# Convolution taps over 1024 tokens instead of two halves, and the forget gate read out by ScalarE, in a one-core hybrid decoder block

## The chip, the core and the metric

The kernel runs on one core of a Trainium2 chip. Its engines work side by side, each through its own queue in order: TensorE (PE; its weight loads are listed as PEld), VectorE (DVE), ScalarE (ACT), GpSimd (POOL), and SyncE (SP), which issues most of the DMAs. The metric is the device time of one execution in microseconds, from 1157.99 to 1163.38 in three runs of the kernel before, with a median of 1163.02.

## What is computed

One layer, 1024 tokens by 1024 features, float32. The part that matters here is the first half of the layer:

```python
h = rms_norm(x, norm1_g)
proj = h @ w_in          # q 512 | k 512 | v 512 | fg 8 | conv_in 512 | pool_in 256
q, k = rms_norm(q per head), rms_norm(k per head)
fg = fg + b_f                                        # forget-gate logits
att = forgetting_attention(q, k, v, fg)              # cumsum(log_sigmoid(fg)) as a bias

a, b = split(conv_in)
c = a * sigmoid(b)                                   # 256 channels
c = causal_depthwise_conv(c, dw_w) + dw_b            # 31 taps
conv = silu(layer_norm(c)) @ pw_w
pool = multiscale_pool(pool_in, pool_w, pool_scale)  # trailing means over 2, 4, 8, 16
x = x + concat[att, conv, pool] @ w_out
```

A gated MLP with 2816 hidden features follows; it takes the larger part of the time and is not touched.

## The kernel before

Features lie on the 128 partitions and tokens along the free axis for the convolution and the pooling; tokens lie on the partitions for q, k, v and the gates. Each product is made of three matmuls of float32 values that were split into a high and a low part (`mm3`, lines 53 to 55). The splits are made by ScalarE (high part, line 48) and by VectorE or GpSimd (low part, line 49).

The first 245 us of the profile go like this:

- Up to about 77 us: loads and splits of the tokens, then the products for the convolution's and the pooling's inputs (512 tokens at a time, `feat_mm`), evacuated by VectorE (`feat_evac`, lines 171 to 182). The gated input of the convolution is `u`, two groups of 128 channels, with 30 zeros ahead of the tokens.
- Then six chunks of `w_in` against all tokens (`tok_chunks`, `tok_mm`): two for v (the second has the 8 gate columns too), then four for q and k. Each chunk has 8 token tiles, and each tile is 8 k blocks by three matmuls into one of four `mm` banks. In the loop over the tiles of chunk ci, `load_w` also loads and splits the weights of chunk ci + 2.
- Beside that, VectorE works at the side work: a generator, `side_work` (line 297), that yields after each step: the taps of channel groups 0 and 1 (`taps`), then the two halves of `conv_tail` (transposes of the finished taps `acc`, layer norm, transposes back, SiLU, split, pointwise product), then `pool_work` (running sums `pn`, then `d`, its split `dhl` and a product). The loops draw it by `step(n)`: 7 steps in each of the eight late feature halves, then 3 after each token tile of the first four chunks; what is left is drained ahead of the fifth.
- In the second chunk each tile's gate logits are read from the bank, scaled by `rstd` and given their bias by one VectorE instruction (line 433). `gate_cumsum` turns them into the cumulative sum `cumx`, which attention needs at its start (line 481).

Two pools are shared. The raw buffers (`rp`, five of them, `raw`) hold the raw weights `wr` of each `load_w`, and also the intermediate tiles of the side work: `y` and `sf` of the conv tails, `pn` and `d` of the pooling, `lf` and `cum` of the gates. The `tp` banks (two) serve the transposes and products of the side work.

The order on each engine is made by a scheduler at build time, from the order in which the code is written, from the dependencies, and from its own timeline. So a step that is drawn earlier is also placed earlier on its engines, and a buffer goes to whoever asks for it earlier in the code.

Of the kernel before, what the change touches and what calls it, by code (L numbers as in the profile page):

```python
# [11 lines left out]
AF = mybir.ActivationFunctionType  # L12
ALU = mybir.AluOpType
# [3 lines left out]
P = 128  # L17
S = 1024
D = 1024
NT = S // P  # L20
KT = D // P
H = 8
# [5 lines left out]
CW = 31  # L28
# [5 lines left out]
PC_G1, PC_CB, PC_LG, PC_LB, PC_PS = 0, 8, 10, 12, 14  # L34
PC_QG, PC_KG, PC_DW, PC_FW, PC_BF = 16, 17, 18, 80, 212
# [4 lines left out]
def tile_hybrid_block(ctx: ExitStack, tc: tile.TileContext, x: bass.AP, xT: bass.AP, prm: bass.AP,  # L40
                      g2: bass.AP, w_in: bass.AP, conv_pw: bass.AP, pool_w: bass.AP, w_out: bass.AP,
                      w_up: bass.AP, w_down: bass.AP, out: bass.AP):
    nc = tc.nc
# [19 lines left out]
    par = const.tile([P, PC_N], F32, name="par")  # L63
    nc.sync.dma_start(out=par, in_=prm)

    def pc(col):
        return par[:, col:col + 1]
# [22 lines left out]
    rstd = const.tile([P, NT], F32, name="rstd")  # L90
# [14 lines left out]
    def raw(shape, name):  # L105
        t = rp.tile([P, 1056], F32, name=name, tag="raw")
        return t[0:shape[0], 0:shape[1]]

    def mmps():
        return pmm.tile([P, 512], F32, name="mm", tag="mm")  # L110

    def tpps():
        return ptp.tile([P, 512], F32, name="tp", tag="tp")
# [18 lines left out]
    def load_w(k, c0, widths, lo=None):  # L132
        n = sum(widths)
        wr = raw((P, n), "wr")
        nc.sync.dma_start(out=wr, in_=w_in[k * P:(k + 1) * P, c0:c0 + n])
        o = 0
        for w in widths:
            t = wp.tile([P, 2, 272], F32R, name="w", tag="w")
            split(t[:, 0, 0:w], t[:, 1, 0:w], wr[:, o:o + w], lo)
            wt[(c0 + o, k)] = t  # L140
            o += w

    mcp = [mxa.tile([P, 4, 512], F32, name=f"mcp{g}", tag="mx") for g in range(2)]
    u = s8.tile([P, 2, 1056], F32, name="u", tag="s8")
    acc = s8.tile([P, 2, 1056], F32, name="acc", tag="s8")
# [8 lines left out]
    fgt = sp.tile([P, NT, H], F32, name="fgt", bufs=1)  # L154
# [92 lines left out]
                yield  # L247

    def taps(c):
        for half in range(2):  # L250
            o = half * 512
            a = acc[:, c, o:o + 512]
            nc.vector.tensor_scalar(out=a, in0=u[:, c, o:o + 512], scalar1=pc(PC_DW + c * CW),
                                    scalar2=pc(PC_CB + c), op0=ALU.mult, op1=ALU.add)
            yield
            for j in range(1, CW):
                nc.vector.scalar_tensor_tensor(out=a, in0=u[:, c, o + j:o + j + 512],  # L257
                                               scalar=pc(PC_DW + c * CW + j), in1=a, op0=ALU.mult, op1=ALU.add)
                yield

    def conv_tail(half):
        o = half * 512
# [34 lines left out]
    def side_work():  # L297
        yield from taps(0)
        yield from taps(1)
        yield from conv_tail(0)  # L300
        yield from conv_tail(1)
        yield from pool_work()
# [3 lines left out]
    def step(n):  # L306
        for _ in range(n):
            next(bg, None)
# [23 lines left out]
    for f in late:  # L332
        for half in range(2):
            ps = mmps()
# [20 lines left out]
    def tok_mm(c0, w, t):  # L355
        ps = mmps()
        ts = slice(t * P, (t + 1) * P)
        for k in range(KT):
            w_ = wt[(c0, k)]
            mm3(ps[:, 0:w], hhi[k][:, ts], hlo[k][:, ts], w_[:, 0, 0:w], w_[:, 1, 0:w], k == 0, k == KT - 1)  # L360
        return ps

    def gate_cumsum():
        fz = sp.tile([P, NT * H], F32, name="fz", bufs=1)
        z = fgt.rearrange("p t h -> p (t h)")
        nc.vector.scalar_tensor_tensor(out=fz, in0=z, scalar=-1.0, in1=z, op0=ALU.mult, op1=ALU.max)
        nc.scalar.activation(out=fz, in_=fz, func=AF.Exp, scale=-1.0)
        nc.vector.tensor_scalar(out=fz, in0=fz, scalar1=1.0, scalar2=None, op0=ALU.add)
        nc.scalar.activation(out=fz, in_=fz, func=AF.Ln)
        nc.vector.scalar_tensor_tensor(out=fz, in0=z, scalar=0.0, in1=fz, op0=ALU.min, op1=ALU.subtract)  # L370
        lf = raw((H, S), "lf")
        for half in range(2):
            ps = tpps()
            for j in range(4):
                t = half * 4 + j
                nc.tensor.transpose(out=ps[0:H, j * P:(j + 1) * P], in_=fz[:, t * H:(t + 1) * H], identity=ident)
            nc.vector.tensor_copy(out=lf[:, half * 512:half * 512 + 512], in_=ps[0:H, :])
        cum = raw((H, S), "cum")
        nc.vector.tensor_tensor_scan(out=cum, data0=lf, data1=lf, initial=0.0, op0=ALU.add, op1=ALU.min)
        nc.vector.memset(cumx.bitcast(F32), 0.0)  # L380
        nc.vector.tensor_copy(out=cumx[0:H], in_=cum)
        nc.vector.tensor_tensor(out=cumx[32:32 + H], in0=cum, in1=cumx[0:H].bitcast(F32), op=ALU.subtract)
# [33 lines left out]
    for ci, (c0, w) in enumerate(tok_chunks):  # L416
        if ci >= 2:
            dst = s8.tile([P, 2112], F32, name="qk", tag="s8")[:, 0:2048].rearrange("p (t c) -> p t c", t=NT)
            qk[ci % 2, (ci - 2) // 2] = dst
        if ci == 4:  # L420
            for _ in bg:
                pass
            pa2.close()
            qkp = qkp_ctx.enter_context(tc.tile_pool(name="qkp", bufs=3, **right))
            bg = prep_pair(0, tpps)
        for t in range(NT):
            ps = tok_mm(c0, w, t)
            if ci + 2 < len(tok_chunks):
                load_w(t, tok_chunks[ci + 2][0], (256,), nc.gpsimd)
            if ci < 2:  # L430
                nc.scalar.activation(out=vv[ci][:, t, :], in_=ps[:, 0:256], func=AF.Copy, scale=rstd[:, t:t + 1])
                if ci == 1:
                    nc.vector.scalar_tensor_tensor(out=fgt[:, t, :], in0=ps[:, 256:264],  # L433
                                                   scalar=rstd[:, t:t + 1],
                                                   in1=par[:, PC_BF:PC_BF + H], op0=ALU.mult, op1=ALU.add)
                step(3)
            else:
                sq = tp_.tile([P, DH], F32, name="sq")
                ss = tp_.tile([P, 4], F32, name="ss")
                for e in range(4):  # L440
                    nc.scalar.activation(out=sq, in_=ps[:, e * DH:(e + 1) * DH], func=AF.Square,
                                         scale=rstd[:, t:t + 1], accum_out=ss[:, e:e + 1])
                rsqrt(ss, ss, DH, 4)
                nc.gpsimd.tensor_scalar(out=ss, in0=ss, scalar1=rstd[:, t:t + 1], scalar2=None, op0=ALU.mult)
                nc.vector.tensor_tensor(out=dst[:, t, :].rearrange("p (h d) -> p h d", d=DH),  # L445
                                        in0=ps[:, 0:256].rearrange("p (h d) -> p h d", d=DH),
                                        in1=ss[:, :, None].broadcast_to([P, 4, DH]), op=ALU.mult)
                step(3 if ci < 4 else 1)
        if ci == 1:
            gate_cumsum()  # L450
# [587 lines left out]
```

## Time and profile before

| | |
|---|---|
| median of three runs | 1163.02 us |
| the profiled execution's own time | 1161.21 us |
| its span | 1159.4 us |
| granted TensorE clock, mean | 0.982 |
| taps (line 257), 120 instructions | 93.3 us busy on VectorE, 49.1 us to 161.0 us |
| first transpose of finished taps (line 267) | 155.0 us |
| first matmul of attention (line 481) | 245.0 us |

In the profile's rows stands first the start in us, then the length in us (in the merged view of time) or the groups' sums, then engine, line, operation, and the tile written, `<-`, the tiles read. `x6` says that six instructions are merged. In square brackets is the engine's idle time just before, and what ended it. A line of 48, 49 or 53 to 55 is that of a helper, so tiles say more than lines there.

### The profile page before, as it was taken

What the parts mean: (1) busy time and instruction counts of PE and PEld (TensorE: products, weight loads), DVE (VectorE), ACT (ScalarE), POOL (GpSimd) and SP (SyncE); (2) the same over time, 40 slices, a digit from 0 to 9 for tenths busy, and PEclk for the clock granted to TensorE, in tenths of its full rate; (3) what the DMA queues carried; (4) which work ended last, traced back from release to release, by engine and by line L of the source; (5) the groups of instructions that cost most, each with busy time, mean ns of one, the idle gap of its engine ahead of it and who ended that gap; (6) DMA issues with size and microseconds to landing.
All of it is one profiled execution on the core that took longest, in us unless ns stands there. A gap on an engine that the chain in (4) does not pass through costs nothing.

```text
span 1159.4 us, 15556 instructions
## 1 busy us (share of the span) xinstructions
PE 1104.9 (95%) x5684; PEld 921.4 (79%) x5684; DVE 882.5 (76%) x1259; ACT 576.0 (50%) x1045; POOL 361.4 (31%) x373
## 2 busy tenths in 40 slices
PE   7999889999999999879999999999999999899996
PEld 6789889978778878758888888888888788688875
DVE  5798974758998756778877888787878755998673
ACT  8322456688998644445443535353535343233331
POOL 1365597867666653101212121212121210000010
PEclk9999999999999999969999999999999999899999
DMA  9220110022111141211222121312221397672372
GB/s 359 72 81 25 40 28 20 15 74 74 55 48 46 47 154 73 109 37 55 89 75 96 68 96 68 105 59 85 79 98 67 117 328 267 240 263 91 128 235 74
DMA packets 51885, 119.99 MB, mean 103 GB/s; under 512 B 6368, under 2 KB 11872, under 8 KB 48992
## 3 DMA queue, kind: packets, MB, share of 16 engines
q1 hardware_dynamic: 46208, 99.06, 25.8%
q0 software_dynamic: 5600, 19.93, 4.3%
q8 instruction: 45, 0.74, 0.3%
q14 instruction: 32, 0.26, 0.1%
HBM read 94.84 MB, written 19.92 MB: 99 GB/s over the span
## 4 chain that ended last, share of the span: by engine, by line
PE 69%; DVE 10%; issue 7%; DMA 5%; ACT 4%; POOL 3%; SPq 1%; POOLq 0%; ACTq 0%; DVEq 0%
PE b L53 12%; PE b L55 12%; PE b L54 12%; PE mm L53 3%; PE mm L55 3%; PE mm L54 3%; DVE dl L49 3%; PE s L499 2%; DVE acc L257 2%; PE t L523 2%; DMA dr<-in_w_down_dram 2%; PE c L53 1%; PE c L55 1%; PE c L54 1%; DMA dr<-gd 1%
## 5 line engine op out<-in xcount | busy, mean ns | idle before, releaser
L814 POOL TENSOR_TENSOR ac<-ac 128x1024 f32<-128x1024 f32 x22 | 61.5, 2793 | 367.9 <-ACT u L795 207.3
L770 DVE SCALAR_TENSOR_TENSOR ac<-u,par,ac 128x1023 f32<-128x1023 f32 x88 | 112.7, 1280 | 9.6 <-ACT ac L768 8.7
L53 PE MATMUL mm<-w,hh 128*128 128x256 f32 (+1 forms) x384 | 110.3, 288 | 8.5 <-DVE qk L445 4.6
L54 PE MATMUL mm<-w,hh 128*128 128x256 f32 (+1 forms) x384 | 109.5, 285 | 0.6 <-POOL w L49 0.6
L55 PE MATMUL mm<-w,hl 128*128 128x256 f32 (+1 forms) x384 | 109.1, 284 | 0.0
L48 ACT CAST wsh<-ws 128x2048 fp32r<-128x2048 f32 x22 | 42.0, 1910 | 123.5 <-PE b L54 123.3
L257 DVE SCALAR_TENSOR_TENSOR acc<-u,par,acc 128x512 f32<-128x512 f32 x120 | 93.3, 835 | 0.0
L49 DVE TENSOR_TENSOR dl<-dr,dh 128x1024 fp32r<-128x1024 f32 (+1 forms) x39 | 65.6, 1684 | 28.0 <-ACT dh L48 24.9
L511 POOL TENSOR_TENSOR p<-p,l 128x896 f32<-128x896 f32 (+3 forms) x64 | 72.6, 1151 | 44.0 <-DVE l L510 37.5
L48 ACT CAST dh<-dr 128x1024 fp32r<-128x1024 f32 (+1 forms) x39 | 54.7, 1401 | 58.4 <-PE y L55 24.7
L53 PEld LDWEIGHTS mm<-w,hh 128*128 128x128 f32 x384 | 73.0, 190 | 10.1 <-DVE fgt L433 4.8
L49 POOL TENSOR_TENSOR w<-wr,w 128x256 fp32r<-128x256 f32 (+1 forms) x56 | 63.9, 1166 | 42.6 <-ACT w L48 42.3
L54 PEld LDWEIGHTS mm<-w,hh 128*128 128x128 f32 x384 | 73.1, 190 | 1.2 <-POOL w L49 0.8
L55 PEld LDWEIGHTS mm<-w,hl 128*128 128x128 f32 x384 | 73.2, 191 | 0.3
L864 POOL DMA_DIRECT2D out_dram<-acc x16 | 8.7, 542 | 206.9 <-DVE acc L860 206.3
L54 PE MATMUL x<-dl,dh 128*128 128x512 f32 x176 | 69.6, 395 | 3.4 <-DVE dl L49 3.4
L55 PE MATMUL x<-dh,dl 128*128 128x512 f32 x176 | 69.3, 394 | 0.0
L768 ACT ACTIVATE ac<-u,par 128x1024 f32<-128x1024 f32 x44 | 50.7, 1152 | 36.3 <-DVE u L805 35.8
L48 ACT CAST dh<-res 128x1024 fp32r<-128x1024 f32 x22 | 23.1, 1051 | 84.2 <-PE y L55 55.7
L49 DVE TENSOR_TENSOR wsl<-ws,wsh 128x2048 fp32r<-128x2048 f32 x22 | 50.4, 2290 | 12.4 <-ACT wsh L48 12.4
L677 DVE TENSOR_TENSOR ws<-wur 128x512 f32<-128x512 f32 x22 | 59.1, 2688 | 0.0
L53 PE MATMUL x<-dh 128*128 128x512 f32 x176 | 54.0, 402 | 5.2 <-DVE acc L860 4.5
(308 smaller groups left out, 3395.1 us busy)
## 6 DMA issues: line engine op xcount, KB each, us to landing
wur<-in_w_up_dram SPq DMA_DIRECT2D x22, 1024.0 KB, 4.9
dr<-in_w_down_dram SPq DMA_DIRECT2D x66, 256.0 KB, 5.1
dr<-gd SPq DMA_DIRECT2D x55, 256.0 KB, 4.3
gd<-ac POOLq DMA_DIRECT2D x22, 512.0 KB, 3.0
res<-gd SPq DMA_DIRECT2D x22, 256.0 KB, 5.6
wr<-in_w_in_dram SPq DMA_DIRECT2D x40, 128.0 KB, 2.1
v<-in_x_dram SPq DMA_DIRECT2D x8, 512.0 KB, 8.4
wor<-in_w_out_dram SPq DMA_DIRECT2D x16, 256.0 KB, 3.0
```

The costliest lines, as they stand in the source:

```text
L48: nc.scalar.copy(out=dst_hi, in_=src)
L49: (lo or nc.vector).tensor_tensor(out=dst_lo, in0=src, in1=dst_hi.bitcast(F32), op=ALU.subtract)
L53: nc.tensor.matmul(ps, a_hi, b_hi, start=first, stop=False, skip_group_check=more)
L54: nc.tensor.matmul(ps, a_hi, b_lo, start=False, stop=False, skip_group_check=more)
L55: nc.tensor.matmul(ps, a_lo, b_hi, start=False, stop=last, skip_group_check=more)
L257: nc.vector.scalar_tensor_tensor(out=a, in0=u[:, c, o + j:o + j + 512], scalar=pc(PC_DW + c * CW + j), in1=a, op0=ALU.mult, op1=ALU.add)
L499: nc.tensor.matmul(ps[:, 0:c1 - c0], qT[:, i * P:(i + 1) * P], part[:, c0:c1], start=b == 0, stop=b == 1 and c1 < n)
L511: nc.gpsimd.tensor_tensor(out=pt[:, 0:n], in0=pt[:, 0:n], in1=l[:, 1:2].broadcast_to([P, n]), op=ALU.mult)
L677: nc.vector.tensor_tensor(out=out, in0=a, in1=b, op=ALU.subtract)
L768: nc.scalar.activation(out=ac, in_=us, func=AF.Copy, scale=pc(w0 + 2))
L770: nc.vector.scalar_tensor_tensor(out=ac[:, j:S], in0=us[:, 0:S - j], scalar=pc(w0 + 2 - j), in1=ac[:, j:S], op0=ALU.mult, op1=ALU.add)
L814: nc.gpsimd.tensor_tensor(out=a[:, 1], in0=a[:, 1], in1=a[:, 0], op=ALU.mult)
```

## The change

The taps of a channel group run over all 1024 tokens at once: one bias step and 30 tap steps for each group, so 62 yields where there were 124. The steps that the loops draw stay as they were. The gate logits are read out by ScalarE without the bias, and `gate_cumsum` adds the bias for all 8 tiles in one VectorE instruction.

```diff
     def taps(c):
-        for half in range(2):
-            o = half * 512
-            a = acc[:, c, o:o + 512]
-            nc.vector.tensor_scalar(out=a, in0=u[:, c, o:o + 512], scalar1=pc(PC_DW + c * CW),
-                                    scalar2=pc(PC_CB + c), op0=ALU.mult, op1=ALU.add)
+        a = acc[:, c, 0:S]
+        nc.vector.tensor_scalar(out=a, in0=u[:, c, 0:S], scalar1=pc(PC_DW + c * CW), scalar2=pc(PC_CB + c),
+                                op0=ALU.mult, op1=ALU.add)
+        yield
+        for j in range(1, CW):
+            nc.vector.scalar_tensor_tensor(out=a, in0=u[:, c, j:j + S], scalar=pc(PC_DW + c * CW + j), in1=a,
+                                           op0=ALU.mult, op1=ALU.add)
             yield
-            for j in range(1, CW):
-                nc.vector.scalar_tensor_tensor(out=a, in0=u[:, c, o + j:o + j + 512],
-                                               scalar=pc(PC_DW + c * CW + j), in1=a, op0=ALU.mult, op1=ALU.add)
-                yield
...
     def gate_cumsum():
         fz = sp.tile([P, NT * H], F32, name="fz", bufs=1)
+        nc.vector.tensor_tensor(out=fgt, in0=fgt, in1=par[:, None, PC_BF:PC_BF + H].broadcast_to([P, NT, H]),
+                                op=ALU.add)
...
                 if ci == 1:
-                    nc.vector.scalar_tensor_tensor(out=fgt[:, t, :], in0=ps[:, 256:264],
-                                                   scalar=rstd[:, t:t + 1],
-                                                   in1=par[:, PC_BF:PC_BF + H], op0=ALU.mult, op1=ALU.add)
+                    nc.scalar.activation(out=fgt[:, t, :], in_=ps[:, 256:264], func=AF.Copy, scale=rstd[:, t:t + 1])
```

Three places show how the order on the engines moves. The first is VectorE, from the last evacuations of the pooling's input (`pu`) to the end of the taps. Before, the unbroken run of 36 half steps was followed by one gate readout after another with four half steps between them:

```order
L181 TENSOR_TENSOR pu<-mm,rb 128x512
L257 SCALAR_TENSOR_TENSOR acc<-u,par,acc 128x512 x7
L181 TENSOR_TENSOR pu<-mm,rb 128x512
L257 SCALAR_TENSOR_TENSOR acc<-u,par,acc 128x512 x36
L433 SCALAR_TENSOR_TENSOR fgt<-mm,rstd,par 128x8
L257 SCALAR_TENSOR_TENSOR acc<-u,par,acc 128x512 x4
L433 SCALAR_TENSOR_TENSOR fgt<-mm,rstd,par 128x8
```

Now the same place has 36 full steps (the lines are those of the changed file), then the bias add, the last five full steps, and at once the layer norm of the first conv tail:

```order
L181 TENSOR_TENSOR pu<-mm,rb 128x512
L255 SCALAR_TENSOR_TENSOR acc<-u,par,acc 128x1024 x36
L363 TENSOR_TENSOR fgt<-fgt,par 128x64
L255 SCALAR_TENSOR_TENSOR acc<-u,par,acc 128x1024
L366 SCALAR_TENSOR_TENSOR fz<-fgt 128x64
L255 SCALAR_TENSOR_TENSOR acc<-u,par,acc 128x1024
L368 TENSOR_SCALAR fz<-fz 128x64
L255 SCALAR_TENSOR_TENSOR acc<-u,par,acc 128x1024
L370 SCALAR_TENSOR_TENSOR fz<-fgt,fz 128x64
L255 SCALAR_TENSOR_TENSOR acc<-u,par,acc 128x1024 x2
L268 BN_STATS st<-tp 128x6 x2
```

The full steps of the two channel groups alternate in the run of 36; the last five are all of group 1. The conv tail came, before, only after six tiles of q had been evacuated.

The second place is TensorE at the third chunk (the first of q), whose weights are `w_825` (k block 0), `w_859`, `w_893` and so on. Before, the chunk's first tile went through its k blocks without a break, and so did six more before the first transpose of taps:

```order
L53 MATMUL mm_1375<-w_825,hh_0_117 128x256
L54 MATMUL mm_1375<-w_825,hh_0_117 128x256
L55 MATMUL mm_1375<-w_825,hl_0_125 128x256
L53 MATMUL mm_1375<-w_859,hh_1_118 128x256
L54 MATMUL mm_1375<-w_859,hh_1_118 128x256
L55 MATMUL mm_1375<-w_859,hl_1_126 128x256
```

Now four tiles (`mm_1572`, `mm_1612`, `mm_1652`, `mm_1692`) go through k blocks 0 to 2, and then come the transposes of the first conv tail (`tp<-acc`), k block 3 (`w_958`), and the tail's transposes back:

```order
L53 MATMUL mm_1692<-w_893,hh_2_119 128x256
L265 MATMUL tp_898<-ident_70,acc_136 128x128
L265 MATMUL tp_909<-ident_70,acc_136 128x128
L54 MATMUL mm_1692<-w_893,hh_2_119 128x256
L55 MATMUL mm_1692<-w_893,hl_2_127 128x256
L265 MATMUL tp_898<-ident_70,acc_136 128x128
L265 MATMUL tp_909<-ident_70,acc_136 128x128
L265 MATMUL tp_920<-ident_70,acc_136 128x128 x2
L265 MATMUL tp_962<-ident_70,acc_136 128x128 x2
L53 MATMUL mm_1572<-w_958,hh_3_120 128x256
L53 MATMUL mm_1612<-w_958,hh_3_120 128x256
```

Both conv tails and the first pooling product now stand among the first four tiles of the chunk; the fifth tile comes behind them. Before, they were spread from the third chunk to the sixth.

The third place is SyncE's queue with the raw weights of the third chunk, k blocks 3 to 7, and the semaphores that each load waits for. Before:

```order
L135 DMA wr_925<-in_w_in_dram 128x256 [waits DMAHW5_49,Pool_49]
L135 DMA wr_959<-in_w_in_dram 128x256 [waits DMAHW6_49,Pool_49]
L135 DMA wr_993<-in_w_in_dram 128x256 [waits DMAHW7_49,Pool_49]
L135 DMA wr_1027<-in_w_in_dram 128x256 [waits DMAHW0_49,Pool_49]
L135 DMA wr_1061<-in_w_in_dram 128x256 [waits DMAHW1_49,Pool_49]
```

Now:

```order
L135 DMA wr_956<-in_w_in_dram 128x256 [waits DMAHW6_49,Pool_49]
L135 DMA wr_1018<-in_w_in_dram 128x256 [waits DMAHW1_49,Pool_49]
L135 DMA wr_1077<-in_w_in_dram 128x256 [waits DMAHW5_49,DVE_49,PE_49]
L135 DMA wr_1141<-in_w_in_dram 128x256 [waits DMAHW7_49,DVE_49]
L135 DMA wr_1200<-in_w_in_dram 128x256 [waits DMAHW4_49,Pool_49]
```

The loads of k blocks 5 and 6 wait for VectorE and TensorE, whose tiles of the conv tail (`y`, `sf`) hold the raw buffers, where all waited for GpSimd's splits before. From attention's first matmul on, the order of every engine is the same but for a few rows.

## The prediction

> **What bounds the kernel now.** I read the busy times, then the stages, then what TensorE waits for, then single instructions around the convolution.
>
> ```profile
> PE 1104.9 (95%) x5684; PEld 921.4 (79%) x5684; DVE 882.5 (76%) x1259; ACT 576.0 (50%) x1045; POOL 361.4 (31%) x373
> ```
>
> TensorE is the bound: 95% of the 1159.4 us span. The execution took 1161.21 us, 1.8 below the median of 1163.02; I work against 1161.2 and add nothing for that difference. Only a change that makes TensorE wait less, or more, can move the time. All that the diff touches lies in the first 245 us, so the stages there come next.
>
> ```profile
> core 0: us, PE busy (x) PEld busy (x) DVE busy (x) ACT busy (x) POOL busy (x), PEclk, DMA share, GB/s
> 77.63:100.60 22.97, 22.39 (x187) 22.18 (x186) 22.97 (x33) 5.20 (x13) 6.22 (x6) 1.00 0.07 19
> 100.60:125.00 24.40, 21.82 (x179) 21.55 (x178) 19.42 (x33) 4.51 (x12) 15.33 (x8) 1.00 0.17 44
> 140.00:155.00 15.00, 12.35 (x92) 11.97 (x91) 14.54 (x28) 8.65 (x39) 11.78 (x14) 0.89 0.01 2
> 190.00:240.00 50.00, 49.55 (x396) 48.25 (x395) 35.14 (x67) 33.38 (x136) 36.92 (x56) 1.00 0.07 17
> ```
>
> Each stage row gives its length, then each engine's busy time, the granted clock and the DMA share. From 77.63 us on TensorE multiplies tokens by six weight chunks, 8 token tiles each, while VectorE runs the taps beside it (22.97 of 22.97 us busy). TensorE itself loses little; the view of waits for 77 to 240 us says to whom:
>
> ```profile
> PE mm L53 <- DVE qk L445: 4.6, 2, 2.7
> PE mm L53 <- DVE fgt L433: 4.0, 3, 2.6
> PE tp L267 <- DVE y L275: 1.4, 1, 1.4
> ```
>
> Total, times and longest: 10.0 us together.
>
> **The change, part by part.** First the taps: 124 steps of 512 tokens become 62 of 1024.
>
> ```profile
> 48.16 0.99 DVE L253 TENSOR_SCALAR acc<-u,par 128x512 f32<-128x512 f32 x2
> ...
> 73.29 6.51 DVE L257 SCALAR_TENSOR_TENSOR acc<-u,par,acc 128x512 f32<-128x512 f32 x6
> ...
> 86.53 23.93 DVE L257 SCALAR_TENSOR_TENSOR acc<-u,par,acc 128x512 f32<-128x512 f32 x36
> ...
> 564.38 1.28 DVE L770 SCALAR_TENSOR_TENSOR ac<-u,par,ac 128x1023 f32<-128x1023 f32 x1
> 565.57 0.68 DVE L784 TENSOR_TENSOR u<-u,b 128x512 f32<-128x512 f32 x1
> ...
> 569.03 2.60 DVE L770 SCALAR_TENSOR_TENSOR ac<-u,par,ac 128x1023 f32<-128x1023 f32 x2
> ```
>
> A half step costs 23.93 / 36 = 0.665 us. The same operation on 1023 elements lets its successor start after 1.19 us (564.38 to 565.57), or takes 1.30 where the second needs the first (2.60 / 2). Two bias steps of halves take 0.99; I leave the one that replaces them at that, and a range of a few tenths for it is lost in the rest. So a full tap saves 2 x 0.665 - 1.19 = 0.14 us, some 8 us of VectorE work over 60 steps. VectorE isn't the bound, so this is worth nothing by itself.
>
> What counts is the place. The side work is drawn by a counted number of steps, and its conv tails now come 62 steps earlier in the program. The rows of the order show it: from the first bias step up to the long unbroken run there were 35 half steps, 35 x 0.665 = 23.3 us, and are now 19 full ones, 19 x 1.19 = 22.6; the rest there is alike. So the run still begins near 86 us. It has 36 steps, before and now, but full ones: 36 x 1.19 = 42.8 us, to about 129 instead of 110.5. Behind it stand the bias add on the gates and five more full steps of one channel, each needing the one before: 5 x 1.30 = 6.5.
>
> GpSimd comes into this too.
>
> ```profile
> 73.46 9.34 POOL L49 TENSOR_TENSOR w<-wr,w 128x256 fp32r<-128x256 f32 x8 [5.56 <-ACT w L48]
> 99.55 11.52 POOL L49 TENSOR_TENSOR w<-wr,w 128x256 fp32r<-128x256 f32 x1 [16.75 <-ACT w L48]
> ```
>
> Eight weight splits beside taps go one to one with them: a tap then takes 6.51 / 6 = 1.085 us, 0.42 more than alone. But the split that comes up at 99.55, in the middle of the unbroken run, ends only at 111.07, just after that run's end at 110.46. So with full steps (i) the eight splits for the first chunk take some 8 x 0.52 = 4.2 us longer, and (ii) the splits of the third chunk's first weights, ready near 105 us, wait until the run ends near 129. Three of them among the last five taps add 3 x 0.42 = 1.3.
>
> ```profile
> 127.81 0.47 ACT L431 ACTIVATE v<-mm,rstd 128x256 f32<-128x256 f32 x1 [0.68 <-PE mm L55]
> ...
> 159.90 1.09 DVE L257 SCALAR_TENSOR_TENSOR acc<-u,par,acc 128x512 f32<-128x512 f32 x1
> ```
>
> TensorE finished the second chunk at 127.8. Without the gate wait (2.6) and with the 4.2 of (i) that is 129.4 now, which the gate add needs: VectorE goes on near 130. **Taps end**: 130 + 6.5 + 1.3 = 138 us, against 161 before. Bounds: 135 (129 + 5 x 1.19, no sharing) and 142 (another 4 us of sharing).
>
> That is earlier, yet TensorE now stands in front of it. In the order, after the third chunk's first three k blocks of four tiles (34 small matmuls, 4 us), the next rows of TensorE are transposes of the finished taps; then k blocks 3 to 7 alternate with both conv tails. The loads of blocks 5 and 6 wait for VectorE and TensorE work of the first tail, since its intermediate tiles sit in the same five buffers as the raw weights. Both loads, and every load behind them in SP's queue, come that much later. Before, all loads of this chunk waited for GpSimd alone, and TensorE had 168 small matmuls of the chunk to do ahead of the first such transpose, and whole tiles between the parts of a tail. Now it does both tails with only 62 small matmuls among them, and the chain of a tail is bare.
>
> ```profile
> 189.25 0.38 PE L267 MATMUL tp<-ident,acc 128*128 128x128 f32 x2
> 199.85 0.49 PE L282 MATMUL tp<-ident,y 128*128 128x128 f32 x3
> 208.52 0.39 PE L55 MATMUL tp<-s__2019,cw_hl 128*128 128x512 f32 x1
> ...
> 211.02 0.68 DVE L294 COPY mcp<-tp 128x512 f32<-128x512 f32 x1
> ...
> 213.33 1.14 ACT L48 CAST dhl<-d 128x512 fp32r<-128x512 f32 x2 [0.41 <-DVE pn L223]
> ...
> 215.27 1.29 DVE L49 TENSOR_TENSOR dhl<-d,dhl 128x512 fp32r<-128x512 f32 x2
> ```
>
> The second tail of before took 189.25 to 211.70, 22.4 us, with readouts of q and k between its parts. My estimate without those is 16: transposes to the last normalised tile 7.5 (9.7 in the rows up to 198.9), transposes back 1, SiLU and split 3, twelve products at 0.23 and the copies 4.5. Upper end 22.4, lower end 13. The second tail can't overlap the first: its transposes need the two banks which the first one's copies release. Then TensorE stands at the first pooling product, whose splits came 7.7 us behind the tail's last product (208.9 to 216.6); I take 5, since the running sums are now begun beside the tail, ends 3 and 7.7. So TensorE gets to the fifth tile of the third chunk at 138 + 32 + 5 = **175 us**.
>
> Where was that point before?
>
> ```profile
> 87.26 0.47 ACT L431 ACTIVATE v<-mm,rstd 128x256 f32<-128x256 f32 x1 [2.38 <-PE mm L55]
> ...
> 98.67 0.48 ACT L431 ACTIVATE v<-mm,rstd 128x256 f32<-128x256 f32 x1 [2.38 <-PE mm L55]
> ...
> L481 PE MATMUL f<-cumx,sel x16: 387/497/498, 245.0 to 355.0; 64*128 64x512 f32 x16
> ```
>
> Five readouts, 87.26 to 98.67, are 4 tiles: 2.85 us each. Attention began at 245.0. From the fifth tile on 28 tiles remain, 79.8 us, and with some 5 for 24 transposes and 8 products that is 85. So before, the same work was done by 160. **The delay is 175 - 160 = 15 us.** The 10.0 us of waits of before is inside the 160, so it has not to be taken off again. Behind this point the orders of all engines agree but for a few rows, so I carry the 15 to the end.
>
> A stop also slows what follows it.
>
> ```profile
> 490.00:500.00 10.00, 4.04 (x14) 2.83 (x15) 9.74 (x14) 7.08 (x8) 0.00 (x0) 0.50 0.00 1
> 500.00:510.00 10.00, 6.12 (x15) 4.24 (x15) 10.00 (x10) 4.45 (x5) 0.00 (x0) 0.50 0.00 0
> ```
>
> Where TensorE was busy 4.04 and 6.12 of 10 us, its granted clock was 0.50. Of TensorE's work in the new gap some 6 us lie on the chain (two times 12 products at 0.23 are 5.5). Half of it at half clock adds 3, all of it 6; I take 3, ends 0 and 6.
>
> [...]
>
> The gate readout: TensorE's bank is now freed by ScalarE alone, and the bias add waits for the eighth read; the five taps stand behind it on VectorE, and TensorE waits for those. ScalarE gets 8 small reads, VectorE loses 8 of 0.216 us and gets one add. I have no row of a 128x8 read on ScalarE; the ends are 0 and the 0.47 us of the 256 wide one, and I take 0.3. It hides in the 2.38 us for which ScalarE waits before each readout; uncovered it would cost 8 x 0.3 = 2.4. The 4.0 us for which TensorE waited on the gate readout goes, but taps and tails are late next, so it is worth nothing.
>
> Sum: 1161.2 + 15 + 3 = **1179**.
>
> **The rivals.** (1) *Faster.* The side work is out of the way early, so that waits go: 4.0 for the gates, 4.6 for q and k, 1.4 for the tail, which would give 1161.2 - 10 = 1151. It decides where TensorE gets to the fifth tile of the third chunk: by 160 there is no loss, by 150 the whole gain. For it speaks that the waits on q and k came beside taps; against it that the taps alone can't end before 135, and that two tails in line behind them leave 12 us each. Chance 0.08. (2) *No difference.* Tails of 13, taps at 135, pooling at 3 give 164, a delay of 4: 1165; or the change shortens VectorE's work and moves nothing else, 1161, which the order speaks against. Chance 0.15. (3) *Worse than my forecast.* Tails at the full 22.4 give 175 + 13 = 188 and 1192; what speaks against it is that no q and k readouts stand between the parts. It is counted inside the forecast's case, at about 0.1 of its 0.77.
>
> **How the numbers follow.** Forecast 1179, chance 0.77. A measurement of this kernel tells about 0.5% from no change, 5.8 us: faster is under 1157.2, slower over 1168.8. The lower end takes in the short tails, 1161.2 + 3 = 1164; the upper end is the long tails, 1192.
>
> **What would show it.** The full step near 1.28 us long; the taps' run from 86 to 129; a GpSimd split of over 20 us in it; taps ending near 138; TensorE waiting from about 130 on for splits, then for the normalised tiles and for pooling's split, 25 to 30 us in all between 125 and 180; clock below 1 there; attention's first matmul at 245 + 18 = 263 instead of 245. If TensorE reaches attention before 250, the tails weren't bare and I am wrong; if it does so at 263 and the end isn't later by the same amount, something behind has absorbed it.

## The result and the profile after

The changed kernel takes 1189.84 us in the median of 4 runs (1186.90 to 1190.16), the kernel before, in the runs beside it, 1162.10: a ratio of 1.0239, with a 95% interval of 1.0208 to 1.0271. It is slower by 27.7 us, where 18 were forecast. The profiled execution took 1189.61 us, with a span of 1187.8 and a mean granted clock of 0.971 (0.982 before).

The page of the profile, busy times and the groups that the change touches (busy us, mean ns of one | idle before them):

```profile
PE 1116.1 (94%) x5684; PEld 929.7 (78%) x5684; DVE 868.8 (73%) x1190; ACT 576.1 (49%) x1053; POOL 372.9 (31%) x373
...
L49 POOL TENSOR_TENSOR w<-wr,w 128x256 fp32r<-128x256 f32 (+1 forms) x56 | 84.3, 1527 | 43.2 <-ACT w L48 42.9
L255 DVE SCALAR_TENSOR_TENSOR acc<-u,par,acc 128x1024 f32<-128x1024 f32 x60 | 80.1, 1388 | 0.1
```

VectorE has 13.7 us less to do than before (882.5), and GpSimd's splits take 20.4 us longer (63.9 before) for the same 56 instructions. The merged view of time, VectorE, then GpSimd, shows why (start, length, instruction, idle before it):

```profile
84.58 43.13 DVE L255 SCALAR_TENSOR_TENSOR acc<-u,par,acc 128x1024 f32<-128x1024 f32 x36
127.64 0.21 DVE L363 TENSOR_TENSOR fgt<-fgt,par 128x64 f32<-128x64 f32 x1
...
133.24 2.60 DVE L255 SCALAR_TENSOR_TENSOR acc<-u,par,acc 128x1024 f32<-128x1024 f32 x2
```

```profile
72.18 12.49 POOL L49 TENSOR_TENSOR w<-wr,w 128x256 fp32r<-128x256 f32 x8 [4.18 <-ACT w L48]
100.87 29.92 POOL L49 TENSOR_TENSOR w<-wr,w 128x256 fp32r<-128x256 f32 x3 [16.20 <-ACT w L48]
139.79 0.72 POOL L49 TENSOR_TENSOR w<-wr,w 128x256 fp32r<-128x256 f32 x1
...
167.62 3.84 POOL L49 TENSOR_TENSOR w<-wr,w 128x256 fp32r<-128x256 f32 x1 [5.41 <-ACT w L48]
```

The run of 36 full steps lasts from 84.58 to 127.7, and no split that starts within it ends before it is over: three splits take 29.92 us, the first of them alone 27.57, to 128.44, where one takes 0.72 with no tap beside it. The taps end at 135.84. The stages behind them (length, busy time of PE, PEld, DVE, ACT, POOL, then granted clock, DMA share, GB/s):

```profile
130.00:140.00 10.00, 7.20 (x36) 6.96 (x37) 7.45 (x13) 2.09 (x4) 2.42 (x7) 0.67 0.05 13
140.00:150.00 10.00, 6.78 (x29) 5.59 (x30) 3.83 (x9) 4.37 (x7) 2.97 (x6) 0.67 0.10 24
150.00:160.00 10.00, 6.51 (x32) 5.21 (x31) 4.43 (x12) 0.41 (x1) 2.25 (x6) 0.84 0.01 5
160.00:170.00 10.00, 6.48 (x34) 5.60 (x34) 6.97 (x13) 2.78 (x5) 4.42 (x6) 0.83 0.05 13
170.00:180.00 10.00, 6.07 (x18) 4.85 (x18) 4.47 (x9) 5.14 (x28) 6.15 (x8) 0.66 0.15 39
180.00:190.00 10.00, 9.68 (x61) 8.78 (x62) 8.94 (x17) 5.53 (x21) 9.55 (x12) 0.83 0.26 66
```

From 130 to 180 TensorE is busy 33 of 50 us, at a clock of 0.66 to 0.84. What it waits for between 77 and 275 us (total, times, longest):

```profile
PE mm L54 <- POOL w L49: 10.4, 6, 3.2
PE tp L265 <- DVE y L273: 5.3, 2, 2.7
PE tp L53 <- ACT s__980 L48: 2.9, 1, 2.9
```

These are GpSimd's splits, the normalised tiles of the tails and the SiLU splits of the first tail: the bare chain of the tails, and weights that come late among them. The first matmuls of the fifth tile of the third chunk, and those of attention:

```profile
182.42 0.41 PE L53 MATMUL mm<-w,hh 128*128 128x256 f32 x1
```

```profile
L479 PE MATMUL f<-cumx,sel x16: 387/494/498, 271.0 to 380.8; 64*128 64x512 f32 x16
```

Attention begins 26.0 us later than before (245.0), and the end comes 28.4 later by the two profiled executions.

### The profile page after: what moved, and what is told of

It is laid out like the page before. It is cut to its first block, busy times and chain, and to the rows that moved or that the text cites. A ratio compares the mean times of both kernels' runs of the same rounds, so it can differ in the third digit from the quotient of the medians.

```text
span 1187.8 us, 15502 instructions
## 1 busy us (share of the span) xinstructions
PE 1116.1 (94%) x5684; PEld 929.7 (78%) x5684; DVE 868.8 (73%) x1190; ACT 576.1 (49%) x1053; POOL 372.9 (31%) x373
## 4 chain that ended last, share of the span: by engine, by line
PE 66%; issue 18%; DVE 6%; ACT 4%; POOL 3%; DMA 2%; SPq 0%; POOLq 0%; ACTq 0%; DVEq 0%
PE b L53 12%; PE b L55 12%; PE b L54 12%; PE mm L54 4%; PE mm L53 4%; PE mm L55 4%; PE s L497 2%; PE t L521 2%; POOL w L49 2%; PE c L53 1%; PE c L55 1%; PE c L54 1%; PE f L53 1%; PE f L55 1%; PE f L54 1%
## 5 line engine op out<-in xcount | busy, mean ns | idle before, releaser
L54 PE MATMUL mm<-w,hh 128*128 128x256 f32 (+1 forms) x384 | 112.1, 293 | 10.4 <-POOL w L49 10.4
L49 POOL TENSOR_TENSOR w<-wr,w 128x256 fp32r<-128x256 f32 (+1 forms) x56 | 84.3, 1527 | 43.2 <-ACT w L48 42.9
L54 PEld LDWEIGHTS mm<-w,hh 128*128 128x128 f32 x384 | 75.6, 197 | 11.9 <-POOL w L49 11.6
L255 DVE SCALAR_TENSOR_TENSOR acc<-u,par,acc 128x1024 f32<-128x1024 f32 x60 | 80.1, 1388 | 0.1
L53 PEld LDWEIGHTS mm<-w,hh 128*128 128x128 f32 x384 | 74.7, 197 | 4.3 <-DVE qk L443 3.3
L55 PEld LDWEIGHTS mm<-w,hl 128*128 128x128 f32 x384 | 75.6, 197 | 0.1
L766 ACT ACTIVATE ac<-u,par 128x1024 f32<-128x1024 f32 x44 | 50.7, 1152 | 31.2 <-DVE u L803 30.7
```

The source lines that it names most:

```text
L49: (lo or nc.vector).tensor_tensor(out=dst_lo, in0=src, in1=dst_hi.bitcast(F32), op=ALU.subtract)
L53: nc.tensor.matmul(ps, a_hi, b_hi, start=first, stop=False, skip_group_check=more)
L54: nc.tensor.matmul(ps, a_hi, b_lo, start=False, stop=False, skip_group_check=more)
L55: nc.tensor.matmul(ps, a_lo, b_hi, start=False, stop=last, skip_group_check=more)
L255: nc.vector.scalar_tensor_tensor(out=a, in0=u[:, c, j:j + S], scalar=pc(PC_DW + c * CW + j), in1=a, op0=ALU.mult, op1=ALU.add)
L766: nc.scalar.activation(out=ac, in_=us, func=AF.Copy, scale=pc(w0 + 2))
```

## The experiments

Three theories stood at the start. **D**: the conv tails, drawn earlier, lie bare in front of TensorE. **P**: the full steps themselves cost the time, since they shut GpSimd out for longer. **G**: the gate readout on ScalarE costs it. The first round showed that D alone isn't enough and brought a fourth, **S**, below. All times are medians; "before" is the kernel before in the same session; "splits moved" means that the low parts of the third chunk's weights are made on VectorE instead of GpSimd.

| kernel | taps | gate readout | tails drawn | us | before | ratio (95%) |
|---|---|---|---|---|---|---|
| the change | full | ScalarE | early | 1189.84 | 1162.10 | 1.0239 (1.0208 to 1.0271) |
| e1 | half | ScalarE | as before | 1176.62 | 1159.60 | 1.0143 (1.0128 to 1.0158) |
| e2 | full | VectorE | early | 1180.06 | 1159.60 | 1.0169 (1.0152 to 1.0186) |
| e3 | full | ScalarE | as before | 1173.70 | 1159.60 | 1.0109 (1.0089 to 1.0130) |
| e4 | half | VectorE | early | 1196.72 | 1159.60 | 1.0310 (1.0290 to 1.0330) |
| e6 | half | ScalarE, VectorE reads too | as before | 1161.76 | 1161.21 | 1.0003 (0.9990 to 1.0016) |
| e7 | half | ScalarE, splits moved | as before | 1156.86 | 1161.21 | 0.9957 (0.9939 to 0.9975) |
| e8 | full | VectorE | as before | 1161.75 | 1161.21 | 0.9995 (0.9978 to 1.0013) |
| e9 | full | ScalarE, splits moved | early | 1186.65 | 1161.21 | 1.0218 (1.0196 to 1.0240) |
| e10 | half | VectorE, splits moved | as before | 1161.23 | 1161.30 | 1.0001 (0.9990 to 1.0013) |
| e11 | full | ScalarE, splits moved | as before | 1158.15 | 1161.30 | 0.9986 (0.9971 to 1.0001) |
| e12 | the change, tail tiles in place | ScalarE | early | 1181.55 | 1161.30 | 1.0175 (1.0153 to 1.0197) |
| e14 | e11, tail tiles in place | ScalarE, splits moved | as before | 1170.61 | 1160.14 | 1.0096 (1.0078 to 1.0113) |

### The parts of the change, one by one

**e1** makes only the second and third hunk of the diff: half steps, gate readout on ScalarE, bias added once.

> The gate readout on ScalarE with its bias added once; the taps stay in halves, and the order of the conv tails stays that of the kernel before. Theory D (the conv tails are drawn 62 steps too early, so that both tails and the first pooling product stand bare between four tiles of the third chunk): this edit has no part in the loss; 1156 to 1163 us, since at most the 4.0 us of gate waits can go. Theory G (the gates on ScalarE, and the bias add that waits for the last of them in front of taps, make the loss): about 1180 or more.

Measured 1176.62, 17 us over the kernel before. This was the surprise: the part of the change that I had held for worth nothing costs more than half of the whole loss, though the tails are drawn where they were before.

**e2** makes only the first hunk: full taps, the old gate readout.

> Taps over 1024 tokens, with the old gate readout on VectorE. The order of the conv tails is that of the changed kernel. Theory D: the whole loss or a little more, 1186 to 1194 us, since gate readouts now wait behind full steps. Theory G: near 1163.

1180.06: slower by 20.5 us, and 6 us below the lower end of what D expected.

**e3** is the changed kernel with an empty draw behind every tap, so that the tails come where they came before:

```diff
         for j in range(1, CW):
             nc.vector.scalar_tensor_tensor(out=a, in0=u[:, c, j:j + S], ...
             yield
+            yield
```

(and the same behind the bias step).

> The changed kernel, but each tap step is drawn twice (an empty draw after it), so that taps take 124 draws as before and the conv tails return to the place in the order which they had before. Theory D: the loss goes, and what is left is the gain of the cheaper taps and of the gate waits, 1150 to 1160 us. Theory P (the full steps hold GpSimd's weight splits off, 29.9 us for one of them, and this makes the loss wherever the tails stand): 1175 or more.

1173.70: half of the loss goes, and 14.1 us stay, which D didn't expect; P's 1175 or more is just missed.

**e4** is the kernel before, its two half steps of one tap issued in one draw: none of the change's instructions, but the tails drawn as early.

```diff
-        for half in range(2):
-            o = half * 512
+        for j in range(CW):
+            for half in range(2):
+                o = half * 512
...
+            yield
```

> The kernel before with its half steps and its old gate readout, but two half steps in one draw, so that taps take 62 draws: no instruction is changed, the tails only come earlier in the order, as in the changed kernel. Theory D: the loss comes without the change itself, 1185 to 1195 us. Theory P: the taps are narrow, so 1165 or less.

1196.72, the slowest of all, 37.1 us over the kernel before and 1.7 above D's range. So the early draw alone makes a loss of this size, with half steps and the old gate readout; attention begins at 278.2. In this kernel TensorE waits for the taps as well, which it doesn't in the change, so its loss isn't that of the tails alone (times and longest as above):

```profile
PE tp L268 <- DVE acc L258: 10.2, 2, 5.4
PE tp L268 <- DVE y L276: 6.3, 3, 3.4
```

D holds, but e1 and e3 have a second loss of 14 to 17 us, with the tails at their old place. Where is it? TensorE's waits of e1, and beside them ScalarE's:

```profile
PE mm L53 <- ACT fgt L435: 21.6, 1, 21.6
```

```profile
ACT w L48 <- POOL w L49: 30.4, 1, 30.4
```

One wait of 21.6 us for the gate readout; and ScalarE, which should do it, stood 30.4 us in front of a weight cast, waiting for GpSimd. ScalarE in the kernel before, then in e1:

```profile
101.52 0.48 ACT L431 ACTIVATE v<-mm,rstd 128x256 f32<-128x256 f32 x1 [0.63 <-PE mm L55]
113.28 0.41 ACT L48 CAST w<-wr 128x256 fp32r<-128x256 f32 x1 [11.28 <-DMA wr<-in_w_in_dram]
114.14 0.90 ACT L48 CAST w<-wr 128x256 fp32r<-128x256 f32 x2 [0.45 <-DMA wr<-in_w_in_dram]
114.94 1.57 ACT L431 ACTIVATE v<-mm,rstd 128x256 f32<-128x256 f32 x4
```

```profile
100.75 0.47 ACT L433 ACTIVATE v<-mm,rstd 128x256 f32<-128x256 f32 x1 [0.63 <-PE mm L55]
131.63 0.40 ACT L48 CAST w<-wr 128x256 fp32r<-128x256 f32 x1 [30.41 <-POOL w L49]
132.52 0.91 ACT L48 CAST w<-wr 128x256 fp32r<-128x256 f32 x2 [0.48 <-DMA wr<-in_w_in_dram]
133.34 0.47 ACT L433 ACTIVATE v<-mm,rstd 128x256 f32<-128x256 f32 x1
```

In both, three casts stand ahead of the next readouts in ScalarE's queue, and the first of them needs a raw buffer that GpSimd must release by a split: SyncE issues the load of that buffer at 111.09 before, 0.02 us behind the end of GpSimd's first split (111.07). The cast follows at 113.28 before and at 131.63 in e1, 2.2 and 2.1 us behind the end of that split (111.07 and 129.51). Before, no readout came from 101.52 to 114.94, 13.4 us; in e1 from 100.75 to 133.34, 32.6 us. The program has four `mm` banks for TensorE's tiles, 4 x 2.85 = 11.4 us of work: the rest is 2.0 and 21.2 us, and it waited 2.6 at the longest before and 21.6 in e1. And GpSimd and VectorE in e1:

```profile
98.78 35.63 POOL L49 TENSOR_TENSOR w<-wr,w 128x256 fp32r<-128x256 f32 x8 [16.73 <-ACT w L48]
```

```profile
85.78 43.14 DVE L257 SCALAR_TENSOR_TENSOR acc<-u,par,acc 128x512 f32<-128x512 f32 x65
147.95 0.35 DVE L365 TENSOR_TENSOR fgt<-fgt,par 128x64 f32<-128x64 f32 x1 [19.03 <-ACT fgt L435]
```

VectorE now makes 65 half steps in one run, to 128.9, where the kernel before had stopped after 36, at 110.46, in front of a gate readout whose bank wasn't ready. Behind that stop GpSimd's first split ended, at 111.07, and all eight were over by 116.03 (99.55 + 16.48). In e3 there is no such stop: a run of 36 full steps from 85.69 to 128.8, 31.00 us for eight splits from 103.24, and one wait of TensorE of 17.1 us for the gate readout.

**Theory S**, then: the old gate readout was a brake. Waiting for each tile, VectorE broke its run of taps, GpSimd came to its splits, raw buffers came free and ScalarE's queue went on. With the readout on ScalarE nothing breaks the run.

### Theory S against G

**e6** is e1 with one VectorE instruction more per tile, which reads a column of the same bank into a tile that nobody uses; ScalarE's readouts and the single bias add stay.

```diff
                     nc.scalar.activation(out=fgt[:, t, :], in_=ps[:, 256:264], func=AF.Copy, scale=rstd[:, t:t + 1])
+                    nc.vector.tensor_copy(out=gcol[:, t:t + 1], in_=ps[:, 256:257])
```

> The kernel with half steps and the gate readout on ScalarE (1176.6), with one more VectorE instruction behind each gate readout: it copies one column of the same TensorE bank to a tile that nobody reads, so that VectorE again waits in the middle of its taps for each of the eight tiles. Theory S (an unbroken run of taps on VectorE keeps GpSimd's splits out, and ScalarE's casts wait for these): the run of 36 half steps ends at 110 and breaks, GpSimd's eight splits that start near 99 take 16 to 18 us instead of 35.6, TensorE's wait of 21.6 us on the gate readout goes, 1158 to 1164. Theory G (ScalarE's own eight small reads, or the bias add that waits for the last of them, cost the time): the reads and the add are unchanged, 1173 to 1180.

1161.76, no different from the kernel before. VectorE and GpSimd in it:

```profile
85.19 23.94 DVE L258 SCALAR_TENSOR_TENSOR acc<-u,par,acc 128x512 f32<-128x512 f32 x36
114.42 0.16 DVE L437 COPY gcol<-mm 128x1 f32<-128x1 f32 x1 [5.30 <-ACT fgt L436]
```

```profile
98.21 16.50 POOL L49 TENSOR_TENSOR w<-wr,w 128x256 fp32r<-128x256 f32 x8 [16.74 <-ACT w L48]
```

An instruction added, whose result nobody reads, takes the 17 us away but for 0.6. G falls: reads and add are as in e1.

**e7** is e1 with the other end of the chain taken away: GpSimd isn't asked for the third chunk's splits.

```diff
-                load_w(t, tok_chunks[ci + 2][0], (256,), nc.gpsimd)
+                load_w(t, tok_chunks[ci + 2][0], (256,), nc.vector if ci == 0 else nc.gpsimd)
```

> Half steps, gate readout on ScalarE, and the low parts of the third chunk's weights subtracted on VectorE instead of GpSimd, in the order of the program between the taps. Theory S: nothing of the third chunk waits for GpSimd any more, the 21.6 us wait goes, 1156 to 1164. Theory G: 1173 to 1180. A rival within S: VectorE reaches these eight subtractions only after its own run of 36 half steps, near 110, and is late by as much as GpSimd was before the change; then 1160 to 1166, no gain over the kernel before.

1156.86: the loss goes, and 4.4 us with it, a ratio of 0.9957 (0.9939 to 0.9975). It is the fastest version here. **e10** tells whether this gain is that of the moved splits: the kernel before with the same one line.

> The kernel before, with nothing changed but the low parts of the third chunk's weights, subtracted on VectorE instead of GpSimd. It tells whether the 4.4 us that half steps, gate on ScalarE and this edit together lie below the kernel before (1156.9 against 1161.2) come from this edit alone or need the gate readout on ScalarE too. In the kernel before TensorE waited for gates (4.0) and for q and k (4.6) in this stretch, not for GpSimd's splits. If the edit alone makes the gain: 1155 to 1158. If the gain is the gate wait that the change removes: 1159 to 1163.

1161.23, no difference: the moved splits alone gain nothing in the total. Where e7's 4.4 us come from stays open. In e10, too, TensorE waits for no gate readout between 77 and 275 us, and its attention begins at 241.5, in e7 at 242.0, in the kernel before at 245.0. Up to there the two are alike; they part behind it.

### Full taps without the two losses

**e8** is e2 with the empty draws of e3: full taps, old gate readout, tails at their old place.

> Full taps, each followed by an empty draw (so that the tails keep the place they had in the kernel before), and the gate readout of before on VectorE. Theory S with D (tails drawn early lie bare): neither is there, the run breaks near 109, 1155 to 1163, and some 0 to 4 us below the kernel before since VectorE has 8 us less to do. Rival W (full steps by themselves keep GpSimd out longer than half ones): 1168 to 1176.

1161.75, no difference (0.9978 to 1.0013). P falls: with the old gate readout, full steps cost nothing by themselves, and the VectorE work that they save brings nothing either. **e11** is e3 with the line of e7, the whole change with both losses taken away.

> The whole change (full taps, gate readout on ScalarE with one bias add), each tap followed by an empty draw so that the tails keep their old place, and the third chunk's low parts on VectorE. Theory S plus D says that these two things were all that the change lost: 1152 to 1160, at or under the kernel before. If the two don't cover it (some other cost of full taps with the gate on ScalarE, as the kernel with empty draws alone still took 1173.7): 1166 to 1175.

1158.15 (0.9971 to 1.0001). From e3 it is 1.2% in the ratios, some 14 us, for eight small subtractions on another engine. D and S together cover the loss of the change when each is removed at its root.

**e9** asks how much of the changed kernel's own loss is S: the same line, but the tails early.

> The changed kernel (1189.8) with the low parts of the third chunk's weights on VectorE instead of GpSimd. Theory S plus D: the tails are still early and bare, but the part of the loss that is GpSimd's, the 10.4 us of TensorE's waits on its splits, goes: 1176 to 1184, about where full taps with the old gate readout stand (1180.1). If the whole loss of the changed kernel is D: 1187 to 1192. If S were all of it: below 1168.

1186.65, above what I expected. Counted from the kernel before of each session, the change loses 27.7, e9 25.4, e2 with the old readout 20.5. So GpSimd's splits are only some 2 us of it in this order, and even that isn't clear of noise (the intervals of the two ratios overlap), though TensorE's waits on them fell from 10.4 us to 2.9: in e9 it waits 5.0 us for the taps, which it didn't in the change, and 5.5 instead of 2.7 for pooling's splits. ScalarE's queue in the changed kernel shows why S is weak there:

```profile
100.38 1.12 ACT L48 CAST w<-wr 128x256 fp32r<-128x256 f32 x3
102.84 0.48 ACT L431 ACTIVATE v<-mm,rstd 128x256 f32<-128x256 f32 x1 [1.34 <-PE mm L55]
...
132.17 0.39 ACT L48 CAST w<-wr 128x256 fp32r<-128x256 f32 x1
```

Only three casts of the third chunk stand ahead of the gate readouts here. Before, and in e1, five and then three more came, and the last three needed buffers that GpSimd had to release; here the fourth stands behind all readouts, at 132.17, and so no readout waits for GpSimd. The other 5 us between e9 and e2 I can't assign.

### Why early tails stand bare

**e12** tests the step of the prediction by which the tails hold up the weights: they share the five raw buffers. It is the changed kernel with the tail's tiles written over the finished taps, which nobody needs any more.

```diff
-        yt = raw((P, S), "y").rearrange("p (t c) -> p t c", t=4)
...
-            nc.vector.tensor_scalar(out=yt[:, t, :], in0=ps[:, 0:256], ...
+            nc.vector.tensor_scalar(out=acc[:, :, o + t * P:o + (t + 1) * P], in0=ps[:, 0:256]...
...
-            sf = raw((P, 512), "sf")
+            sf = acc[:, c, o:o + 512]
```

> The changed kernel with the conv tails' tiles (the normalised tokens and the SiLU output) written in place into the finished taps, so that they no longer sit in the five buffers of the raw weights. If it is the sharing of these buffers that puts the tails ahead of the third chunk's weights: TensorE isn't stopped there, the fifth tile of the third chunk is reached by 160 instead of 182, and the tails go between whole tiles. But in the order of this kernel the rest of the second tail, all of pooling and the gate transposes now stand together at the end of the fourth chunk, in front of the first preparation of heads; there the same bare chain of some 16 us for the tail and a few for pooling comes, so the total stays 1172 to 1190 with the stop at 230 to 260. If that chain is done by the other engines beforehand: 1158 to 1168. If the fifth tile is still reached at 175 or later, the sharing wasn't the reason.

The readout of the fifth tile of the third chunk on VectorE, and the stages of e12 (columns as above):

```profile
155.60 0.42 DVE L443 TENSOR_TENSOR qk<-mm,ss 128x256 f32<-128x256 f32 x1 [0.20 <-POOL ss L442]
```

```profile
150.00:160.00 10.00, 9.50 (x81) 9.29 (x80) 8.14 (x11) 7.01 (x37) 8.75 (x15) 1.00 0.05 15
160.00:170.00 10.00, 10.00 (x87) 10.00 (x86) 6.00 (x16) 5.08 (x26) 7.99 (x16) 1.00 0.01 2
...
180.00:190.00 10.00, 6.92 (x46) 5.82 (x45) 4.99 (x13) 3.71 (x20) 5.89 (x13) 0.99 0.00 0
190.00:200.00 10.00, 7.27 (x20) 5.33 (x20) 4.16 (x9) 3.31 (x5) 1.62 (x5) 0.50 0.01 2
...
220.00:230.00 10.00, 3.85 (x20) 3.67 (x20) 4.27 (x7) 8.77 (x39) 6.96 (x15) 0.70 0.05 15
```

That tile is read out at 155.60, 27 us before TensorE even starts on it in the changed kernel. The stop from 130 to 180 has shrunk to the first 20 us (8.47 and 6.54 us busy in the slices from 130 and 140): TensorE is busy 9.50 of 10 us from 150 and all of it from 160, at full clock. It comes back from 180 on, with the clock at 0.50 from 190, where the second tail now stands in one piece, from 185.38 to 200.31. The total is 1181.55, 20.3 us over the kernel before. The first half of the expectation held: without the shared buffers the tails don't hold up the fifth tile. Of the second half the range held, not the reason in full: the stop was expected at 230 to 260, and beside the one bare tail stand 11.6 us of waits for q and k readouts, the longest of them 6.2 us up to 226.61. Writing in place also let the running sums of pooling in between the taps, so e12 differs in VectorE's order too.

**e14** puts the same in-place tiles into e11.

> The whole change with empty draws and the third chunk's low parts on VectorE (1158.2), and in it the conv tails' tiles written in place into the finished taps, so that no tail tile holds a buffer of the raw weights. TensorE's waits left in that kernel between 77 and 285 us were 3.4 on the tails' tiles and 2.9 on GpSimd's weight splits; if in-place tiles take the first of them away, 1152 to 1157, under the kernel before; if VectorE's and ScalarE's turns and not the buffers set those waits, 1156 to 1162.

1170.61, 0.96% over the kernel before: a miss, worse than both cases. TensorE is busy 7.54 and 5.79 us in the two slices from 190 to 210 there, around the second tail (10.00 in both in e11). Between 180 and 220 us it waits 2.2 us for the tail's normalised tiles, 2.0 for q and k readouts and 2.5 for pooling's tiles, where e11 has no wait. Freeing the buffers moved the side work on VectorE; why the scheduler's order came out so wasn't followed up.

## Why the prediction was right, and where it wasn't

**The mechanism held**: the tails come early and bare. e4 makes a loss from the draws alone, and e8 shows that without them, and with the old gate readout, full taps lose nothing.

**Taps**: the run was forecast from 86 to 129 and went from 84.58 to 127.7; a split of over 20 us was forecast, and the first took 27.57; the end of the taps was put at 138, bounds 135 to 142, and came at 135.84.

**The first tail** was 16 and took 17.3: from its first transpose at 136.51 to the end of its last product at 153.82. **Pooling**, 5, took 4.8 (177.59 to 182.42).

**The second tail is the term that was mis-sized**: 16 forecast, 23.0 measured, from its first transpose (154.62) to the end of its last product (177.59). That is even a little over the 22.4 of the upper bound, which I had put aside because no q and k readouts stand in the tail. Something else does:

```profile
154.62 0.60 PE L265 MATMUL tp<-ident,acc 128*128 128x128 f32 x4
...
166.77 0.73 PE L53 MATMUL tp<-s__1154,cw_hl 128*128 128x512 f32 x2 [1.61 <-ACT s__1154 L48]
173.39 0.63 PE L54 MATMUL tp<-s__1154,cw_hl 128*128 128x512 f32 x1
173.81 0.63 PE L55 MATMUL tp<-s__1154,cw_hl 128*128 128x512 f32 x1
...
177.19 0.40 PE L55 MATMUL tp<-s__1164,cw_hl 128*128 128x512 f32 x1
```

Between its second and its third product lie 6 us, in which TensorE has third-chunk matmuls to do, and these wait 3.2 us for the split that took 3.84 from 167.62, beside VectorE's own SiLU split and its work for the pooling; and the products behind it follow each other at 0.43 instead of 0.23 us. I had counted the weight blocks between the tails as 62 matmuls, not as blocks that can wait for a split. Two other runs bear this out: the second tail takes 15.2 us in e9 (152.33 to 167.50), where VectorE makes these splits, and 17.1 in e2 (155.13 to 172.27), where the same block's split takes 1.02 us.

**The clock** was the other term too small: 3, ends 0 and 6. Busy time times what is missing from full clock, over the six slices from 130 to 190, is 2.4 + 2.2 + 1.0 + 1.1 + 2.1 + 1.6 = 10.4 us, an estimate (the chunk's 128x256 matmuls start 0.21 us apart at a clock of 0.50 and 0.12 at 1.00); not all of it is on the chain. In turn TensorE's plain waits were fewer: 17.4 us between 125 and 180 (7.4 for splits, 5.3 and 0.2 for normalised tiles, 2.9 and 1.6 for SiLU splits) and 2.7 for pooling's split, which ended at 180.32, so 20.1 and not 25 to 30. Waits and clock were one loss, and I split it wrongly. The 0.66 to 0.84 of the slices are means: in slices of 1 us the clock goes between 1.00 and 0.50, and it is at 0.50 in six stretches between 129 and 184 us, three of about 3.4 and three of about 6.8 us, some 30.7 us together; the 3 of the forecast is half of some 6 us of work on the chain at that clock.

The sum: the fifth tile at 182.42 instead of 175, so 7.4 late. The second tail is 7.0 of it; the first tail's 1.3 and two gaps, 1.5 together, stand against taps that ended 2.2 early and pooling's 0.2, so these misses nearly cancel, by luck. That time has the slow clock in it already, so 182.4 - 160 = 22.4 stands against the 15 + 3 = 18 forecast. Attention came 26.0 later, 3.6 more than that, and the end 28.4; the last 2.4 are less than single runs of the kernel before differ by.

**The gate step failed**, and by e2 it holds most of the miss: full taps with the old readout lose 20.5 us where 18 were forecast, and the whole change 27.7. Of these 7.2 us the second tail, 5.8 us shorter in e2, is the part that was seen; the rest wasn't traced. "Worth nothing" was argued from ScalarE's side alone, and that side was right: a readout takes 0.26 us (0.3 estimated) and hides in the wait. What I never asked is what the old instruction did on the engine that lost it. On VectorE it was the break behind the first 36 half steps, and e1 with e6 shows that break to be worth some 16 us at the old place of the tails. I had even quoted the row that shows it, a GpSimd split that ended just behind the run, and drew from it only that a longer run makes a longer wait. The remark that the 4.0 us of gate waits is worth nothing stays undecided: e7 is 4.4 us faster than the kernel before, but e10, where TensorE doesn't wait for gates either, isn't.

**VectorE's saved work** (8 us by my count, by the starts of the taps; 13.7 in the busy times, where taps overlap) is worth nothing: right, e8.

## What to carry to other kernels

Where side work is drawn by a count of steps, a change of the step's size moves everything behind it; repace the draws with the size. Before an instruction that waits is taken off an engine, ask who got through while it waited: here an unbroken run of taps on VectorE held a GpSimd split for 30.73 us, and over buffers and ScalarE's queue TensorE waited 21.6 us (e1). Where that happens, small subtractions that a later stage needs are safer on the engine that makes the run than on the one that it shuts out (e7 against e1: 1156.86 and 1176.62; e11 against e3: 1158.15 and 1173.70; with the tails early, e9 against the change, it gave next to nothing: 1186.65 and 1189.84).

## What the hardware showed

A GpSimd subtraction of 128x256 took 0.72 us with no tap beside it (at 139.79 in the changed kernel). In VectorE's long run of back-to-back taps the first one to start was over only behind the end of the run: it took 11.52 us before (run to 110.46, split to 111.07), 27.57 in the changed kernel (127.7 and 128.44) and 30.73 in e1 (128.9 and 129.51). The one of e1, from 98.78 to 129.51, sat through some 45 of the 65 half steps ((128.9 - 98.8) / 0.664).

Not beside every run did a split take so long. One that came up at 73.46 before took 1.16 us, one at 72.18 in the changed kernel 1.69, and the next ones went one to one with the taps. What makes the difference isn't shown. In e4 the run was broken at 109.20 by a gate readout on VectorE, 0.22 us long, with no wait in front of it; taps followed from 109.34 to 113.38. There three splits that began at 98.35 were over at 112.17.

TensorE's granted clock in the changed kernel was 0.50 from 129.34 to 136.16, 139.58 to 142.99, 146.40 to 153.22, 160.06 to 163.46, 170.30 to 177.12 and 180.54 to 183.94 us, and 1.00 between these. With the time from 125.93 to 183.94 cut into 17 stretches of about 3.41 us, half the length of the longer ones, the full clock was followed by half behind stretches in which TensorE was busy 0.68 to 1.68 us, and by full behind 1.81 and 2.00; the half clock was followed by half behind 1.95 to 2.60 us, and by full behind 2.97 to 3.41. Why the clock changes isn't shown.
